# A two-layer decoder trunk on one core: two pairs begun in the first token half instead of one, and half of the affine steps moved to the down stage

## The chip, the core and the metric

The kernel runs on one core of a Trainium2 chip. The metric is the device time of one execution in microseconds (us). TensorE (PE) multiplies matrices into eight accumulator banks; VectorE (DVE) and ScalarE (ACT) read these banks and prepare operands; GpSimd (POOL), SyncE (SP) and ScalarE issue DMAs. Each engine works through its own instructions in order.

## The reference, cut

The input x has 512 tokens of width 1024. Each of two layers mixes tokens (layer 0 by pooling, layer 1 by differential attention) and then runs a gated feed-forward network of inner width 2816.

```
for i in range(DEPTH):                                   # DEPTH = 2
    h = _multiscale_pool(...) if i % 2 == 0 else _diff_attention(...)
    x = _layernorm(ALPHA * x + h, ln_mix_g[i], ln_mix_b[i])
    x = _layernorm(ALPHA * x + _swiglu(x, w_gate[i], w_up[i], w_down[i]), ln_ffn_g[i], ln_ffn_b[i])

def _swiglu(x, w_gate, w_up, w_down):
    return (jax.nn.silu(x @ w_gate) * (x @ w_up)) @ w_down
```

## The kernel before, in words

Every float32 operand is split in two: a **high part**, rounded by a cast on ScalarE (line 670 for gate and up weights), and a **low part**, the rest, taken by a subtraction on VectorE (line 673). Each product is three matmuls: high by high, high by low, low by high. Both parts of a weight chunk of 128x1024 lie in one of six buffer pairs (`WBUFS`), and the raw chunk before it in one of five (`RAWS`); SyncE loads raw chunks in the order of `rows_of_wall`.

The function `ffn(layer, late)` has a gate stage and a down stage.

**Gate stage.** The 2816 inner columns are 22 features of 128. Feature rows k and k + 11 make pair k. Pairs 0 to 2 are computed as six plain features f = 0 to 5, each with a gate product g and an up product u: 24 matmuls of 512 tokens each (lines 160 to 162), or 48 of 256 tokens if the feature is done in two token halves. Pairs 3 to 10 (`SPLIT`) go through `strassen(k)`: seven half products P1, Q5, P6, Q3, P7, P2, Q4 of 24 matmuls of 256 columns (line 877), in place of eight. They work on three banks: A takes P1, P6, P7 and Q4 in turn, C takes Q5 and Q3, B takes P2. Between two of them a bank must be read: P1 is copied from A to B, Q5 from C (line 975) and P6 from A (line 977) by ScalarE; Q3 (line 979) and P7 (line 981) are taken by VectorE. So Q3 waits for the copy of Q5, P7 for the copy of P6, and Q4 for the subtraction of P7. Then follow the gate (silu) and two multiplications into the tile `hid` (lines 994, 995).

The left operands of the seven products are quarters of x or sums of them; `sums_of_x` makes these sums in eight steps that use free rows of `hid`. Four of the seven weight operands are sums of raw chunks (line 667). `ahead(j + n)` writes, after product j, the casts and low parts of all chunks up to j + n - 1; n is the look-ahead.

Two more kinds of work are spread over the gate stage for later. `weight_sums` adds the raw down weights of one feature pair (lines 781, 782), which GpSimd loaded and partly accumulated (lines 775, 776), and ScalarE stores them (line 786). `sum_hidden(k)` makes the sums of `hid` that the down stage needs (lines 807 to 814: four operations of 256 columns, a cast and a low part, then a store). Both are put into the list `behind`, from which `catch_up` takes one step after each product. A pair in `SPARED` has its `sum_hidden` put behind a later pair: {2: 6, 3: 8}.

The first token half of x is ready before the second. A layer therefore begins with products that need only the first half: g and u of the first `EARLY[layer]` features (two in layer 0, one in layer 1), then P1 and P2 of pair 3, which is therefore called **begun** and later has only five products (P6, Q5, P7, Q3, Q4). Among these first products stand the transpositions of the last token blocks (`late`). Then the same features are done for the second half, and the rest follows: the remaining plain features up to 5, then pairs 3 to 10.

The previous layer norm is finished lazily: `affine(n - 1, f)` multiplies a token block of the residual by the norm's gain and adds its bias (lines 238, 239), two VectorE instructions of 1024 columns, behind features 0 to 3. The gain and bias rows lie in a tile of tag `gb`, which afterwards holds down weights of odd pairs.

**Down stage.** The same seven products, in six items each (line 1034, 512 columns), with weights and left operands prepared four and five items ahead. P6 and Q3 add to the second half of the columns of token blocks 0 and 1, P1 and P2 to the first; Q5 and P7 to the second half of blocks 2 and 3, Q4 to the first.

Of the kernel before, what the change touches and what calls it, by code (L numbers as in the profile page):

```python
# [18 lines left out]
P = 128  # L19
S = 512  # L20
# [29 lines left out]
EARLY = (2, 1)  # L50
GATE = ("P1", "Q5", "P6", "Q3", "P7", "P2", "Q4")
SPARED = {2: 6, 3: 8}
# [5 lines left out]
def trunk(ctx, tc, x, wall, pscale, lam_p, subln, table, lng, lnb, band, first, onehot, out):  # L58
# [41 lines left out]
    def rows_of_ffn(layer, c):  # L100
        g = list(range(c, c + 2 * FB))
        e, pair = 2 * EARLY[layer], c + 4 * SPLIT[0]
        return g[:e] + [pair, pair + 3] + g[e:] + list(range(c + 2 * FB, c + 3 * FB))
# [131 lines left out]
    def affine(n, s):  # L235
        z = res[:, s, :]
        gb = gbs[n]
        nc.vector.tensor_tensor(z, z, gb[:, 0, :], op=ALU.mult)
        nc.vector.tensor_tensor(z, z, gb[:, 1, :], op=ALU.add)
# [305 lines left out]
    def ffn(layer, late):  # L545
# [3 lines left out]
        c1 = c0 + 2 * FB + 2  # L549
        down = rows_of_wall[c0] + 2 * FB  # L550
        early = EARLY[layer]
        tt = nc.vector.tensor_tensor
        with tc.tile_pool(name=f"ffn{layer}", bufs=1) as fp:
# [64 lines left out]
            def row(c):  # L618
                return c0 + c + (2 if c >= 2 * early else 0)

            for f in range(2 * SPLIT[0]):
                for i in range(2):
                    plain_chunk((f, i), row(2 * f + i))
                if f == early - 1:
                    plain_chunk((SPLIT[0], 0, "pair"), c0 + 2 * early)
                    plain_chunk((SPLIT[0], 5, "pair"), c0 + 2 * early + 1)
            for k in SPLIT:
                c = [row(4 * k + i) for i in range(4)]
                todo = [(c[0], ()), (c[0], (c[0], c[1])), (c[0], (c[0], c[2])), (c[2], ())]
                todo += [(c[1], (c[1], c[2])), (c[3], ()), (c[0], (c[0], c[3]))]  # L630
                begun = k == SPLIT[0]
# [13 lines left out]
                for w in order_of.split(", "):  # L645
                    steps.append((w[:-2], number[k, int(w[-1]), "pair"]))
            uses = {}
# [68 lines left out]
            def sums_of_x():  # L716

                r0, r1, r2, r3 = spare(4), spare(15), spare(6), spare(17)
# [178 lines left out]
            g3 = fp.tile([P, S], F32, name=f"g3_{layer}")  # L897
            ready_first = 2 * early + 2
            for lo in (0, 256):
                for f in range(early):  # L900
                    for i in range(2):
# [6 lines left out]
                        if not lo and (f, i) in late:  # L908
                            late[f, i]()
# [10 lines left out]
                if not lo:  # L920
                    bankA, bankB = bank(f"A{layer}_{SPLIT[0]}"), bank(f"B{layer}")
                    half_product(bankA, number[SPLIT[0], 0, "pair"], lefts["P1"], True, False, True)
                    if "P1" in late:
                        late["P1"]()
                    nc.scalar.copy(both(g3), both(bankA))
                    next(sums)
                    half_product(bankB, number[SPLIT[0], 5, "pair"], lefts["P2"], True, True)
                    tt(both(g3), both(bankB), both(g3), op=ALU.add)
                    next(sums)

            def plain(f):
# [3 lines left out]
                for i in range(2):  # L935
                    product(a[i], j + i, 0, S)
                    ahead(j + i + 5)
                    if f >= 3:
                        next(sums, None)
                    catch_up()  # L940
                gated(order[f], *a)
                if f < SB:
                    affine(n - 1, f)
                if f % 2:
# [6 lines left out]
            def strassen(k):  # L951
                names = {"P1": "A", "P6": "A", "P7": "A", "Q4": "A", "Q5": "C", "Q3": "C", "P2": "B"}
                begun = k == SPLIT[0]
                banks = {"A": bankA if begun else bank(f"A{layer}_{k}"), "C": bank(f"C{layer}_{k}")}
# [7 lines left out]
                if begun:  # L962
                    g0 = g3
                    nc.scalar.activation(g0, g0, AF.Silu)
                for p in BEGUN if begun else GATE:
# [12 lines left out]
                    elif p == "Q3":  # L978
                        tt(first, acc, first, op=ALU.subtract)  # L979
# [21 lines left out]
            f = early  # L1001
            while f < FB:
                if f // 2 in SPLIT:
                    strassen(f // 2)
                    f += 2
                else:
                    plain(f)
                    f += 1
            if final:
                load_gb(n)  # L1010

# [32 lines left out]
            for p in DOWN:  # L1044
# [7 lines left out]
                for i in range(together):  # L1052
# [13 lines left out]
                    multiply(j, accs, range(2))  # L1066
                for s in range(2):
# [466 lines left out]
    ffn(0, {(1, 0): later(0, 2), "P1": later(0, 3)})  # L1534
    attention()
    ffn(1, {(0, 1): later(2, 3)})
# [108 lines left out]
```

## Time and profile before

| what | value |
|---|---|
| runs | 943.16, 941.47, 939.94 us; median 941.47 |
| profiled execution | 938.56 us |
| its span | 936.8 us |
| granted TensorE clock, mean | 0.998 |
| HBM read, written | 175.50 MB, 36.72 MB |
| gate stage of layer 0, from its first feature to the end of pair 10 | 31.95 to 265.24 us |
| gate stage of layer 1 | 593.33 to 823.79 us |

The span runs from the first to the last instruction of the profiled execution; what lies around it is start and end. Times in the views are microseconds from the span's start unless they are marked ns. A group's row gives the busy time, the mean of one instruction, and the idle time of the engine before it with what ended it.

### The profile page before, as it was taken

The numbers are of one execution on the slowest core, as the hardware profiler recorded it, in microseconds if no ns is written. First come the engines' busy times: TensorE is split into PE (matmuls) and PEld (weight loads), VectorE is DVE, ScalarE is ACT, GpSimd is POOL, SyncE is SP. The second block draws the span as 40 slices with busy tenths as digits, with TensorE's granted clock in tenths as the row PEclk, the third lists the DMA queues.
The fourth block names the chain that finished last, engine by engine and source line by source line (L and its number), as shares of the span: only waits on it lengthen the run. The fifth ranks groups of instructions, "written<-read, shape, count | busy, mean of one in ns | idle before, by whom it ended". The sixth has DMA issues, their size and how long they took to land. (4 is left out here: it accounts for less than half of the span.)

```text
span 936.8 us, 15062 instructions
## 1 busy us (share of the span) xinstructions
PE 923.9 (99%) x5758; PEld 828.1 (88%) x5758; DVE 801.2 (86%) x1172; ACT 517.6 (55%) x826; POOL 127.1 (14%) x152
## 2 busy tenths in 40 slices
PE   9999999999999999999999999999999999999996
PEld 8998899999988888888888888988999999988885
DVE  7979899999988787868989776878899999987778
ACT  6652445544564457676878854833354454564450
POOL 4121111110101201201111100211121110001101
PEclk9999999999999999999999999999999999999999
DMA  8497888886778988966666622595888885888942
GB/s 228 165 307 241 219 294 291 252 272 218 249 247 263 368 265 236 224 198 157 157 146 166 162 79 68 146 343 165 257 281 262 274 263 201 263 285 280 359 163 90
DMA packets 86614, 213.21 MB, mean 228 GB/s; under 512 B 15204, under 2 KB 26724, under 8 KB 86542
## 3 DMA queue, kind: packets, MB, share of 16 engines
q1 hardware_dynamic: 43996, 119.26, 38.2%
q0 software_dynamic: 18768, 58.20, 25.0%
q10 hardware_dynamic: 23778, 34.78, 10.1%
q8 instruction: 45, 0.74, 0.3%
q14 instruction: 27, 0.22, 0.1%
HBM read 175.50 MB, written 36.72 MB: 227 GB/s over the span
## 5 line engine op out<-in xcount | busy, mean ns | idle before, releaser
L667 DVE TENSOR_TENSOR raw<-raw,raw 128x1024 f32<-128x1024 f32 x64 | 78.2, 1222 | 1.5 <-DMA raw<-in_wall 0.5
L134 ACT CAST xs<-hid 128x512 fp32r<-128x512 f32 (+1 forms) x60 | 34.5, 582 | 24.3 <-DVE hid L844 24.3
L135 DVE TENSOR_TENSOR xs<-hid,xs 128x512 fp32r<-128x512 f32 (+1 forms) x60 | 38.3, 642 | 7.8 <-ACT xs L134 7.8
L1273 ACT ACTIVATE p<-p,mn 128x128 f32<-128x128 f32 (+3 forms) x64 | 35.3, 552 | 14.1 <-DVE mn L1268 14.1
L260 ACT ACTIVATE y<-pt,bT,gT 128x128 f32<-128x128 f32 x72 | 27.1, 456 | 24.5 <-PE pt L246 18.5
L775 POOL DMA_DIRECT2D b<-in_wall x20 | 14.0, 705 | 179.6 <-DMA tsum<-b 83.3
L836 POOL DMA_DIRECT2D xs<-ssum x24 | 17.4, 725 | 138.6 <-PE Q L1034 117.4
L975 ACT COPY hid<-C 128x512 f32<-128x512 f32 x16 | 9.4, 588 | 43.7 <-DVE u L807 17.9
L210 POOL TENSOR_TENSOR rs<-rs,mhalf 128x1 f32<-128x1 f32 x16 | 12.9, 806 | 142.1 <-DVE rs L209 97.5
L1268 DVE CUSTOM_DVE_ANT_0 p<-s,bias 128x128 f32<-128x128 f32 (+3 forms) x64 | 28.0, 485 | 1.1 <-PE s L1253 1.1
L775 POOL DMA_DIRECT2D hid<-in_wall x24 | 19.4, 852 | 64.5 <-DMA tsum<-hid 32.5
L724 ACT CAST xs<-hid 128x1024 fp32r<-128x1024 f32 x8 | 8.4, 1051 | 28.0 <-DVE hid L736 17.1
L201 DVE BATCH_NORM_STATS2 st<-res 128x6 f32<-128x512 f32 x32 | 22.2, 694 | 1.1
L135 DVE TENSOR_TENSOR xt<-y,xt 128x512 fp32r<-128x512 f32 x18 | 12.2, 689 | 10.7 <-ACT xt L134 10.7
L776 POOL DMA_DIRECT2D hid<-in_wall x12 | 14.8, 1233 | 48.3 <-DMA hid<-in_wall 48.3
L812 ACT CAST v<-u 128x512 fp32r<-128x512 f32 x22 | 13.6, 616 | 10.7 <-DVE u L810 10.7
L776 POOL DMA_DIRECT2D b<-in_wall x10 | 12.3, 1230 | 51.4 <-DMA b<-in_wall 44.5
L1287 DVE SCALAR_TENSOR_TENSOR p<-p,sm,p 128x128 f32<-128x128 f32 (+3 forms) x32 | 17.7, 552 | 1.1
L979 DVE TENSOR_TENSOR hid<-C,hid 128x512 f32<-128x512 f32 x16 | 11.0, 689 | 8.6 <-PE C L877 8.6
L708 DVE TENSOR_TENSOR hid<-sg,u 128x512 f32<-128x512 f32 x12 | 8.2, 686 | 11.6 <-PE u L162 6.3
L135 POOL TENSOR_TENSOR sql<-sq,sqh 128x512 fp32r<-128x512 f32 x7 | 9.3, 1323 | 60.5 <-ACT sqh L134 60.5
L814 DVE TENSOR_TENSOR v<-u,v 128x512 fp32r<-128x512 f32 x22 | 15.1, 686 | 1.4 <-ACT v L812 0.7
(1220 smaller groups left out, 3627.3 us busy)
## 6 DMA issues: line engine op xcount, KB each, us to landing
raw<-in_wall SPq DMA_DIRECT2D x126, 512.0 KB, 5.1
r<-tsum SPq DMA_DIRECT2D x40, 512.0 KB, 4.5
hid<-in_wall POOLq DMA_DIRECT2D x36, 512.0 KB, 7.8
b<-in_wall POOLq DMA_DIRECT2D x30, 512.0 KB, 7.4
r<-in_wall SPq DMA_DIRECT2D x30, 512.0 KB, 5.7
tsum<-hid ACTq DMA_DIRECT2D x24, 512.0 KB, 5.0
ssum<-v ACTq DMA_DIRECT2D x22, 512.0 KB, 5.2
tsum<-b ACTq DMA_DIRECT2D x20, 512.0 KB, 4.3
```

The source lines that it names most:

```text
L134: nc.scalar.copy(dst_h, src)
L135: (low or nc.vector).tensor_tensor(dst_l, src, dst_h.bitcast(F32), op=ALU.subtract)
L201: nc.vector.bn_stats(stats[n, s][:, d, :], res[:, s, d * 512 : (d + 1) * 512])
L260: nc.scalar.activation(y[:, k, :], pt[:, k * P : (k + 1) * P], AF.Identity, bias=bT[:, n, kk : kk + 1], scale=gT[:, n, kk : kk + 1],)
L667: tt(t, raws[pair[0]], raws[pair[1]], op=ALU.add)
L775: nc.gpsimd.dma_start(out=t[:, j], in_=src[:, j])
L776: nc.gpsimd.dma_start(out=t[:, 0], in_=src[:, :, 1], accum_op=ALU.add)
L814: tt(v[:, :, 1, :], u, v[:, :, 0, :].bitcast(F32), op=ALU.subtract)
L836: nc.gpsimd.dma_start(out=t.bitcast(F32), in_=ssum[:, 0 if p == "P7" else 1, :, r, :])
L1268: nc.vector.tensor_tensor_reduce(out=p, in0=accs[c], in1=biases[h][:, w - 1 :: -1] if w < S else biases[h][:, ::-1], op0=ALU.add, op1=ALU. ...
L1273: nc.scalar.activation(p, p, AF.Exp, bias=mn[:, q, c : c + 1], scale=-1.0, accum_out=sm[:, q, c : c + 1],)
L1287: nc.vector.scalar_tensor_tensor(p0[:, r], p0[:, r], sm[:, q, 0:1], p1[:, r], op0=ALU.mult, op1=ALU.add)
```

## The change

Of the first products, one feature is taken out and one pair put in. `EARLY` becomes (1, 0), and `PRE` = pairs 3 and 4 are both begun: layer 0 starts with g and u of feature 0, then P1 and P2 of pair 3, then of pair 4; layer 1 starts with the four half products of the two pairs alone. P2 of a begun pair now also does all its high parts first. The order behind them is written out: features 0 to 4, pair 3, feature 5, pairs 4 to 10. Features that were halved (feature 1 in layer 0, feature 0 in layer 1) are plain ones now.

`affine` takes half of the columns in the gate stage; the other halves come behind two items of P6 and two of Q3. For that, the gain and bias rows are loaded a second time at the end of the gate stage, and in layer 1 the rows of the last norm are loaded behind the last of these steps instead. The sums of x begin at feature 2 instead of 3 and use rows one lower, so that they share none with the terms of pair 1. The look-ahead becomes 4 in begun pairs and 6 from pair 6 on; the spared sums are those of pairs 3 and 4, put behind pairs 7 and 10, in place of 2 and 3 behind 6 and 8.

```
-EARLY = (2, 1)
+EARLY = (1, 0)
+PRE = SPLIT[:2]
+SUMS = 2
+SPARED = {3: 7, 4: 10}
+ORDER = "f0 f1 f2 f3 f4 p3 f5 p4 p5 p6 p7 p8 p9 p10".split()
+def lookahead(k, p):
+    return 4 if k in PRE else 6 if k > 5 else 4 if p in ("P1", "Q5", "P6") else 5
+AFFINE = {("P6", 2): (0, 1), ("P6", 3): (1, 1), ("Q3", 1): (2, 0), ("Q3", 2): (3, 0)}
-SPARED = {2: 6, 3: 8}
...
-    def affine(n, s):
-        z = res[:, s, :]
+    def affine(n, s, d=None):
+        c = slice(0, D) if d is None else slice(d * 512, (d + 1) * 512)
+        z = res[:, s, c]
...
-                r0, r1, r2, r3 = spare(4), spare(15), spare(6), spare(17)
+                r0, r1, r2, r3 = spare(3), spare(14), spare(5), spare(16)
...
-                    t = rows_of[:, :, 4:6, :]
+                    t = rows_of[:, :, 7:9, :]
...
-            ready_first = 2 * early + 2
+            ready_first = 2 * early + 2 * len(PRE) + (early == 0)
...
                 if not lo:
-                    bankA, bankB = bank(f"A{layer}_{SPLIT[0]}"), bank(f"B{layer}")
-                    half_product(bankA, number[SPLIT[0], 0, "pair"], lefts["P1"], True, False, True)
...
+                    for k in PRE:
+                        pre_a[k], b = bank(f"A{layer}_{k}"), bank(f"B{layer}_{k}")
+                        g = both(pre_g[k])
+                        half_product(pre_a[k], number[k, 0, "pair"], lefts["P1"], True, False, True)
+                        advance(ready_first, True)
+                        turn_late()
+                        nc.scalar.copy(g, both(pre_a[k]))
+                        half_product(b, number[k, 5, "pair"], lefts["P2"], True, True, True)
+                        turn_late()
+                        tt(g, both(b), g, op=ALU.add)
+                        next(sums)
+                    bankB = b
...
-                    product(a[i], j + i, 0, S)
+                    product(a[i], j + i, 0, S, by_part if f == i == 0 else None)
+                    if f >= SUMS:
+                        next(sums, None)
                     ahead(j + i + 5)
-                    if f >= 3:
-                        next(sums, None)
...
-                    affine(n - 1, f)
+                    affine(n - 1, f, f // 2)
-                if f % 2:
+                if f % 2 or f == 0:
                     weight_sums()
...
-                    ahead(j + (4 if begun or p in ("P1", "Q5", "P6") else 5 if k < SPLIT[-1] else 6))
+                    ahead(j + lookahead(k, p))
                     catch_up()
-                    if p == "Q3" and k in SPARED.values():
+                    if p == "Q3":
                         behind.extend(sum_hidden(i) for i in SPARED if SPARED[i] == k)
...
-            if final:
-                load_gb(n)
-
+            load_gb(n - 1)
             while behind:
                 catch_up()
...
                     multiply(j, accs, range(2))
+                    if (p, i) in AFFINE:
+                        affine(n - 1, *AFFINE[p, i])
+                        if final and (p, i) == list(AFFINE)[-1]:
+                            load_gb(n)
...
-    ffn(0, {(1, 0): later(0, 2), "P1": later(0, 3)})
+    ffn(0, {3: later(0, 2), 5: later(0, 3)})
     attention()
-    ffn(1, {(0, 1): later(2, 3)})
+    ffn(1, {2: later(2, 3)})
```

How the instructions move is shown at three places. The first is TensorE at the beginning of layer 0's gate stage; `w2` to `g_5` are weight chunks (h and l their parts), `A_3` and `B_3` the banks of pair 3, `pt` a transposition. Before:

```order
L690 MATMUL u_0_542<-xt,w3h 128x256 x16
L690 MATMUL u_0_542<-xt,w3l 128x256 x8
L690 MATMUL g_1_543<-xt,w4h 128x256 x16
L690 MATMUL g_1_543<-xt,w4l 128x256 x8
L246 MATMUL pt_2_0_630<-ident,res 128x128 x4
L246 MATMUL pt_2_1_631<-ident,res 128x128 x4
L690 MATMUL u_1_544<-xt,w5h 128x256 x16
L690 MATMUL u_1_544<-xt,w5l 128x256 x8
L877 MATMUL A_3_678<-xt,w6h 128x256 x16
L877 MATMUL A_3_678<-xt,w6l 128x256 x8
```

The same place after the change:

```order
L719 MATMUL u_0_542<-xt,w3h 128x256 x16
L719 MATMUL u_0_542<-xt,w3l 128x256 x8
L906 MATMUL A_3_605<-xt,w4h 128x256 x16
L906 MATMUL A_3_605<-xt,w4l 128x256 x8
L266 MATMUL pt_2_0_631<-ident,res 128x128 x4
L266 MATMUL pt_2_1_632<-ident,res 128x128 x4
L906 MATMUL B_3_606<-xt,w5h 128x256 x16
L906 MATMUL B_3_606<-xt,w5l 128x256 x8
L906 MATMUL A_4_682<-xt,w6h 128x256 x16
L906 MATMUL A_4_682<-xt,w6l 128x256 x8
```

The first half of feature 1 gave its place to P1 and P2 of pair 3, and pair 3 its place to pair 4; the transpositions stand where they stood.

The second place is VectorE in pair 7 of layer 0, from the low part of a sum of hidden rows (`v`) to the subtraction of P7 (`A_7`); `C_7` is the bank of Q3. Before:

```order
L814 TENSOR_TENSOR v_6_2124<-u_6_2123,v_6_2124 128x2x256
L979 TENSOR_TENSOR hid_537<-C_7_2090,hid_537 128x2x256
L673 TENSOR_TENSOR g_46l<-raw_1739,g_46h 128x1024
L673 TENSOR_TENSOR g_47l<-raw_1976,g_47h 128x1024
L981 TENSOR_TENSOR hid_537<-hid_537,A_7_2089 128x2x256
```

After the change:

```order
L843 TENSOR_TENSOR v_6_2084<-u_6_2083,v_6_2084 128x2x256
L1019 TENSOR_TENSOR hid_537<-C_7_2048,hid_537 128x2x256
L696 TENSOR_TENSOR raw_1908<-raw_1908,raw_1980 128x1024
L696 TENSOR_TENSOR raw_1980<-raw_1980,raw_2074 128x1024
L702 TENSOR_TENSOR g_48l<-raw_1908,g_48h 128x1024
L1021 TENSOR_TENSOR hid_537<-hid_537,A_7_2047 128x2x256
```

The low parts g_46l and g_47l now come before Q3 is taken, and two sums and a low part of pair 8 stand between Q3 and P7.

The third place is VectorE at the same point of pair 10, the last; `d` are down weights, `xs` a left operand of the down stage. Before:

```order
L979 TENSOR_TENSOR hid_537<-C_10_2810,hid_537 128x2x256
L673 TENSOR_TENSOR g_67l<-raw_2457,g_67h 128x1024
L135 TENSOR_TENSOR d_0l<-r_0_2704,d_0h 128x1024
L135 TENSOR_TENSOR d_1l<-r_1_2775,d_1h 128x1024
L135 TENSOR_TENSOR xs_538<-hid_537,xs_538 128x512 x2
L981 TENSOR_TENSOR hid_537<-hid_537,A_10_2809 128x2x256
```

After the change:

```order
L1019 TENSOR_TENSOR hid_537<-C_10_2767,hid_537 128x2x256
L154 TENSOR_TENSOR d_1l<-r_1_2699,d_1h 128x1024
L154 TENSOR_TENSOR xs_538<-hid_537,xs_538 128x512
L1021 TENSOR_TENSOR hid_537<-hid_537,A_10_2766 128x2x256
L154 TENSOR_TENSOR d_2l<-r_2_2793,d_2h 128x1024
L154 TENSOR_TENSOR xs_538<-hid_537,xs_538 128x512
L836 TENSOR_TENSOR u_4_2934<-hid_537 128x256
L837 TENSOR_TENSOR hid_537<-hid_537 128x256
```

The low parts g_67l and d_0l are made before Q3 is taken; the spared sum of pair 4 (`u_4`) stands behind P7's subtraction.

More of the change, by code (lines that the diff above doesn't have):

```diff
@@ L100, in rows_of_ffn @@
     def rows_of_ffn(layer, c):
-        g = list(range(c, c + 2 * FB))
-        e, pair = 2 * EARLY[layer], c + 4 * SPLIT[0]
-        return g[:e] + [pair, pair + 3] + g[e:] + list(range(c + 2 * FB, c + 3 * FB))
+        g = list(range(c, c + 2 * EARLY[layer]))
+        g += [c + 4 * k + i for k in PRE for i in (0, 3)]
+        for kind, i in units(layer):
+            g += [c + 2 * i + j for j in range(2)] if kind == "f" else [c + 4 * i + j for j in range(4)]
+        return g + list(range(c + 2 * FB, c + 3 * FB))
     order_of_rows = (
@@ L616, in plain_chunk, with rows, plain_chunks, pair_chunks @@
                 step("low", number[key])
[L618 to L628, printed above, removed]
+            row = [c0]
+            def rows(count):
+                row[0] += count
+                return range(row[0] - count, row[0])
+            def plain_chunks(f):
+                for i, c in enumerate(rows(2)):
+                    plain_chunk((f, i), c)
+            def pair_chunks(k):
+                c = rows(4)
                 todo = [(c[0], ()), (c[0], (c[0], c[1])), (c[0], (c[0], c[2])), (c[2], ())]
                 todo += [(c[1], (c[1], c[2])), (c[3], ()), (c[0], (c[0], c[3]))]
-                begun = k == SPLIT[0]
+                begun = k in PRE
                 for p in BEGUN if begun else GATE:
@@ L646, in ffn @@
                     steps.append((w[:-2], number[k, int(w[-1]), "pair"]))
+            for f in range(early):
+                plain_chunks(f)
+            for k in PRE:
+                for m, c in zip((0, 5), rows(2)):
+                    plain_chunk((k, m, "pair"), c)
+            for kind, i in units(layer):
+                (plain_chunks if kind == "f" else pair_chunks)(i)
             uses = {}
```

53 lines of the change are left out of this document (25 added, 28 removed).

## The prediction

> **What bounds the kernel now.** I read the head of the page first, for how full the engines are.
>
> ```profile
> span 936.8 us, 15062 instructions
> PE 923.9 (99%) x5758; PEld 828.1 (88%) x5758; DVE 801.2 (86%) x1172; ACT 517.6 (55%) x826; POOL 127.1 (14%) x152
> ```
>
> TensorE is full, and its granted clock is 1.00 in every stretch shown below. So time can only go where matmuls are removed or made cheaper, or where TensorE waits. The second view is the busy time by stretches. I cut it at the first matmul of each pair as the timeline shows them: layer 0 has pair 3 from 106.87, pair 4 from 121.90 and so on to pair 10, then two stretches of the down stage (Q5's and P6's multiplications); layer 1 has pairs 3, 4, 7, 9 and 10. Columns: length, then busy time and instructions of PE, PEld, DVE, ACT, POOL, the clock, the DMA share and GB/s.
>
> ```profile
> 106.87:121.90 15.03, 14.98 (x121) 14.54 (x120) 13.75 (x16) 4.44 (x8) 1.24 (x1) 1.00 0.96 293
> 121.90:142.89 20.99, 20.41 (x170) 20.21 (x169) 19.93 (x21) 11.64 (x14) 4.17 (x5) 1.00 0.87 281
> 142.89:163.05 20.16, 20.16 (x170) 20.16 (x169) 18.68 (x23) 10.09 (x13) 2.70 (x3) 1.00 0.92 290
> ...
> 183.20:203.80 20.60, 20.44 (x171) 20.24 (x170) 20.39 (x25) 10.53 (x14) 1.91 (x3) 1.00 0.88 273
> ...
> 223.95:244.53 20.58, 20.42 (x171) 20.21 (x170) 20.37 (x25) 10.53 (x14) 2.35 (x3) 1.00 0.70 251
> 244.53:265.24 20.71, 20.41 (x170) 20.21 (x169) 19.66 (x26) 12.66 (x18) 0.00 (x0) 1.00 0.81 254
> 295.19:310.15 14.96, 14.96 (x68) 12.39 (x66) 11.65 (x16) 7.92 (x11) 4.34 (x6) 1.00 0.91 318
> 310.15:325.11 14.96, 14.96 (x68) 12.39 (x66) 9.26 (x11) 5.39 (x7) 3.61 (x5) 1.00 1.00 373
> ...
> 665.98:680.37 14.39, 14.39 (x121) 14.39 (x120) 13.05 (x15) 5.00 (x7) 1.23 (x1) 1.00 0.98 307
> 680.37:700.74 20.37, 20.37 (x171) 20.21 (x169) 18.82 (x20) 11.01 (x14) 4.28 (x6) 1.00 0.86 284
> 741.06:761.63 20.57, 20.41 (x170) 20.20 (x169) 20.36 (x25) 10.60 (x14) 2.70 (x3) 1.00 0.79 255
> 781.79:802.37 20.58, 20.42 (x171) 20.21 (x170) 20.37 (x25) 10.51 (x14) 1.99 (x3) 1.00 0.70 238
> 802.37:823.79 21.42, 20.67 (x171) 20.27 (x170) 19.58 (x26) 12.65 (x18) 0.33 (x1) 1.00 0.80 257
> ```
>
> An undisturbed pair lasts 20.16 us: 7 products of 24 matmuls, 168 in all (the x170 counts neighbours at the borders). What a pair lasts beyond 20.16 (a begun pair of five products: 14.39) is TensorE waiting. In the gate stages that is 0.64 + 0.83 + 0.44 + 0.42 + 0.55 = 2.88 us in layer 0 and 0.21 + 0.41 + 0.42 + 1.26 = 2.30 us in layer 1. The rows also say why: VectorE has 18.7 us of work in a normal pair, and 20.4 in pairs 7 and 9, which follow a spared sum (put behind pairs 6 and 8). VectorE is second in line, with 1.4 us of air per pair. The waits view names whom TensorE waited for:
>
> ```profile
> PE A L877 <- DVE hid L981: 0.9, 2, 0.6
> PE A L877 <- ACT hid L977: 0.8, 5, 0.2
> PE C L877 <- ACT hid L975: 0.6, 1, 0.6
> ```
>
> All are releases of an accumulator bank: VectorE's subtraction of P7 (L981) before Q4, and ScalarE's copies (L977, L975). ScalarE itself is half idle; its copies are late because its queue waits for VectorE, as around pair 7 of layer 0:
>
> ```profile
> 192.95 1.05 ACT L670 CAST g_46h<-raw 128x1024 fp32r<-128x1024 f32 x1 [0.78 <-DVE raw L667]
> 193.90 0.62 ACT L812 CAST v<-u 128x512 fp32r<-128x512 f32 x1
> 194.42 0.58 ACT L977 COPY hid<-A 128x512 f32<-128x512 f32 x1
> ```
>
> The copy of P6 stands behind a cast that waited for VectorE's sum of raw weights.
>
> **The change, part by part.** *Halved features.* The first loop of a layer still has six half products in layer 0 and four in layer 1, and the two transpositions stand at the same places among them. But one feature per layer is now computed on all 512 tokens in 48 matmuls, not in 96 of 256 columns. The wide price is from the chain:
>
> ```profile
> 868.86 14.96 PE Q L1034 x66
> ```
>
> 14.96 / 66 = 226.7 ns for 512 columns; 20.16 / 168 = 120.0 ns for 256. Two narrow ones cost 13.3 ns more than a wide one, and 96 such couples go (48 in each layer): **−1.28 us**, on TensorE itself, so nothing hides it. The Trainium skill, TensorE: Matmul & The Clock Gate, Back-to-back issue gap, gives a warm gap of N / 2.4 ns plus 2.5 ns, by which a couple would save only 2.5 ns; as an estimate from that page the term would be −0.24 us and the forecast 1.04 us later. The rows decide, since they are this kernel's own matmuls with their weight loads.
>
> New weights are wanted 5.8 us earlier after the loop. In layer 1 the first full feature starts where the second half of the first feature started before (first row), and needs the last cast of x (second row):
>
> ```profile
> 605.79 0.28 PE L160 MATMUL g<-xt,w102h 128*128 128x256 f32 x1
> ```
> ```profile
> 603.40 0.62 ACT L134 CAST xt<-y 128x512 fp32r<-128x512 f32 x1
> 603.92 0.58 ACT L925 COPY g<-A 128x512 f32<-128x512 f32 x1
> 604.40 1.05 ACT L670 CAST g_4h<-raw 128x1024 fp32r<-128x1024 f32 x1
> ```
>
> One copy and one weight cast, such as the last two rows (0.58 and 1.05), now precede the casts of x. Even if nothing hides them, the last cast ends 1.63 us later, at 605.65, before 605.79: cost 0. One cast more in front of it would cost 0.9.
>
> *Half of the affine steps.* An affine step has two instructions on 1024 columns; the price of a half is that of the nearest 512-column operation (second row; the third is needed below):
>
> ```profile
> L238 DVE TENSOR_TENSOR res<-res,gb x12: 1217/1220/1221, 59.5 to 646.4; 128x1024 f32<-128x1024 f32 x12
> ```
> ```profile
> 188.18 0.68 DVE L995 TENSOR_TENSOR hid<-sg,hid 128x512 f32<-128x512 f32 x1
> ...
> 190.11 0.42 DVE L807 TENSOR_TENSOR u<-hid 128x256 f32<-128x256 f32 x1
> ```
>
> Before, each gate stage held 8 x 1.22 = 9.8 us of it. Now it holds 8 x 0.68 = 5.4, and the down stage 5.4: 2.7 in P6's multiplication (11.65 becomes 14.4 of 14.96) and 2.7 in Q3's (9.26 becomes 12.0). Weights and left operands are prepared four items of 2.7 us ahead, so I cost this at 0; if that lead is gone, each step holds TensorE by its 1.4 us, 5.4 per layer. The affine rows are loaded once more per layer on SP's queue, in front of down-stage fetches. Those are as far ahead, so 0 too.
>
> *Sums one feature sooner, and a feature between the begun pairs.* In layer 0 VectorE was late for pair 3. Relieved of 4.3 us of affine work and with the sums started a feature earlier, it should have all operands ready: **−0.64**. Behind the begun pair stood pair 4 with 0.83 and 0.21; now it is pair 5 that follows a begun pair, without air in its weights. What held it was this order:
>
> ```profile
> 129.51 0.69 DVE L782 TENSOR_TENSOR hid<-hid 128x512 f32<-128x512 f32 x1
> 130.23 0.37 ACTq L786 DMA_DIRECT2D tsum<-hid  x1
> 130.64 0.59 ACT L975 COPY hid<-C 128x512 f32<-128x512 f32 x1 [3.74 <-DVE hid L782]
> ```
>
> The same order stands in pair 5. VectorE should come there about 0.6 us earlier against TensorE, because a plain feature now stands between the begun pairs, whose 10.9 us hold only two low parts, a gate, a sum of terms and one of hidden rows on VectorE (2.4 + 0.7 + 1.4 + 2.4 = 6.9). I leave 0.2 per layer: −1.04 + 0.4 = **−0.64**.
>
> *Look-ahead of 6 from pair 6 on, spared sums at 7 and 10.* ScalarE's copies now stand ahead of the casts that need new sums, so the pattern of pair 7 goes. Pairs 7 and 9: 0.44 + 0.42 + 0.41 + 0.42 = **−1.69**. In pair 10 the subtraction that Q4 waits for stood behind the low parts g_67l, d_0l, d_1l and two of left operands; now only d_1l and one of a left operand (1.22 + 0.68) stand between it and Q3's. **−1.81**. Against that: in every later pair two sums and one low part now stand between VectorE's evacuation of Q3 and of P7. Their price is here:
>
> ```profile
> 178.31 2.48 DVE L667 TENSOR_TENSOR raw<-raw,raw 128x1024 f32<-128x1024 f32 x2
> 180.71 1.22 DVE L673 TENSOR_TENSOR g_41l<-raw,g_41h 128x1024 fp32r<-128x1024 f32 x1
> ```
> ```profile
> 134.52 0.69 DVE L979 TENSOR_TENSOR hid<-C,hid 128x512 f32<-128x512 f32 x1 [0.92 <-PE C L877]
> ```
>
> From Q3's end (TensorE begins P7 at 134.25): evacuation from +0.27 to +0.96, the three operations to +4.5, P7's subtraction to +5.1, and Q4 is due at +5.76. So 0.5 us of slack is left after 0.15 for the signal. Before, only two low parts (2.3 us) stood there, so the slack was 1.7. Pair 6 gets three more operations (3.6 us) where the look-ahead deepens; 1.4 of air and 1.7 of slack take 3.1, so up to 0.5 can be left: I put +0.3 per layer. Pair 8 follows a spared sum (4 x 0.42 + 0.68 = 2.4 us) with 1.4 of air and 0.5 of slack, so up to 0.5: +0.2 per layer. Together **+1.0**; bounds 0 and 2.0.
>
> Sum: −1.28 − 0.64 − 0.64 − 1.69 − 1.81 + 1.0 = **−5.06 us**. The profiled execution took 938.56 us, its span 936.8 and 1.8 around it; it would become 933.5. It lies 2.9 below the median of the three runs, so from 941.47 the forecast is **936.4 us**.
>
> **The rivals.** *The waits move and do not go.* VectorE's total work hardly falls, so air lost in one pair may return in the next: pairs 5, 6, 8 and 10 of both layers wait about 0.6 each (4.8 us) in place of the 4.54 that pairs 4, 7, 9 and 10 wait now. Left are 1.28 and 0.64, less 0.3: −1.7, **939.8**. For it speaks that a spared pair's 20.4 us of VectorE exceed 20.16, and that pair 10 (19.66) now gets 2.4 more; against it, that VectorE has air in the first features.
>
> *The terms of the last pair are late anyway.* The edit doesn't do what its new order promises if a DMA sets the pace in pair 10:
>
> ```profile
> 801.49 6.42 DMA b<-in_wall
> ```
>
> The chain that ended last begins with this load, which landed at 807.9, 5.5 us into pair 10; VectorE stood before it in order. It now reaches it two operations (2.3 us) later, so most of the wait should be covered. If not, 1.3 remain: −3.8, **937.7**.
>
> *Slower.* The 0.5 us of slack at P7's subtraction fails in all of pairs 6 to 10, because the low part between must await ScalarE's cast of the fresh sum, and that queue holds a v cast and a copy (0.62 + 0.58). With 1.5 us more there, each of 10 pairs waits 1.0: −1.28 − 0.64 − 0.64 − 3.50 + 10 = +3.9, **945.4**. It turns slower from 0.61 us per pair. Against it: at 178.31 the second sum covered the cast and VectorE had no gap.
>
> **How the numbers follow.** Forecast 0.58, moving waits 0.20, late terms 0.10, slower 0.12. The range leaves out the slower case and a little at the fast end: 934.0 (all waits in the gate stages gone, 1.28 + 5.18, and another 1 us of scatter among runs) to 940.9 (the moving waits, with 1.1 for the bounds of the new order). About 0.3%, 2.8 us, can be told from no change here. The forecast and most of the late terms lie beyond it: faster 0.66. The moving waits with the rest: same 0.22. Slower 0.12.
>
> **What would show it.** TensorE should have 96 matmuls fewer, and the second feature of layer 0 and the first of layer 1 should run at 227 ns a matmul. Pair 3 of layer 0 should last 14.4, pairs 7, 9 and 10 about 20.2, pairs 5, 6 and 8 20.2 to 20.5. TensorE should no longer wait for the subtraction of P7 in pair 10. Down-stage multiplications should stay at 14.96. The forecast is wrong if a pair from 6 on lasts over 20.8, if the first full feature of layer 1 starts after 606, or if P6's or Q3's stage grows.

## The result and the profile after

The changed kernel takes **948.68 us** (median of 22 runs, 941.40 to 955.61); the kernel before, on the same chip, 942.63 us (22 runs, 937.83 to 947.88). The ratio is 1.0061, 95% interval 1.0039 to 1.0083: slower by about 5.7 us, where 5 us faster was forecast. The runs also lie further apart than before.

The head of the page of the changed kernel, whose profiled execution took 949.09 us:

```profile
span 947.3 us, 14914 instructions
PE 926.9 (98%) x5662; PEld 824.0 (87%) x5662; DVE 803.5 (85%) x1190; ACT 518.7 (55%) x826; POOL 127.3 (13%) x152
```

The 96 matmuls are gone (5758 to 5662), yet the span is 10.5 us longer. That is more than the medians show, since the profiled execution of before lay 4.1 us under the median of its 22 runs. Busy time by stretches, cut as for the kernel before, in layer 0: pair 3, feature 5, then pairs 4, 5, 6, 7 and 10, then the multiplications of P1, Q5 and P6:

```profile
101.24:115.63 14.39, 14.39 (x121) 14.39 (x120) 11.87 (x15) 5.65 (x8) 3.21 (x4) 1.00 1.02 315
115.63:126.54 10.91, 10.91 (x51) 9.02 (x49) 6.75 (x7) 4.59 (x5) 0.73 (x1) 1.00 0.89 292
126.54:141.38 14.84, 14.62 (x122) 14.45 (x120) 13.54 (x19) 4.82 (x7) 2.64 (x4) 1.00 0.82 290
141.38:162.97 21.59, 20.66 (x170) 20.26 (x169) 20.28 (x21) 11.83 (x14) 4.25 (x6) 1.00 1.00 303
162.97:184.05 21.08, 20.64 (x170) 20.27 (x169) 20.55 (x25) 11.69 (x15) 3.94 (x4) 1.00 0.97 290
184.05:204.21 20.16, 20.16 (x170) 20.16 (x169) 19.18 (x24) 9.82 (x12) 2.70 (x3) 1.00 0.87 263
...
244.71:265.40 20.69, 20.40 (x170) 20.20 (x169) 17.07 (x25) 10.74 (x15) 0.00 (x0) 1.00 0.83 254
265.40:283.49 18.09, 15.55 (x69) 12.25 (x68) 11.31 (x18) 7.92 (x13) 0.00 (x0) 1.00 0.68 220
283.49:298.86 15.37, 15.27 (x68) 12.31 (x66) 14.00 (x19) 8.82 (x14) 0.75 (x1) 1.00 0.73 239
298.86:314.11 15.25, 15.25 (x67) 12.24 (x66) 11.91 (x17) 7.55 (x11) 4.35 (x6) 1.00 0.92 324
```

The same view in layer 1: pairs 4, 5 and 6, then pair 10, P1 and Q5:

```profile
689.50:704.24 14.74, 14.62 (x122) 14.45 (x121) 13.43 (x19) 4.82 (x7) 3.46 (x4) 1.00 0.82 295
704.24:725.84 21.60, 20.67 (x171) 20.26 (x170) 20.35 (x21) 11.83 (x14) 3.44 (x4) 1.00 1.04 330
725.84:746.56 20.72, 20.63 (x171) 20.27 (x170) 20.49 (x25) 11.75 (x15) 3.93 (x4) 1.00 0.82 257
...
807.22:829.22 22.00, 20.67 (x171) 20.27 (x170) 17.07 (x25) 10.73 (x15) 0.00 (x0) 1.00 0.79 241
829.22:847.71 18.49, 15.60 (x68) 12.23 (x67) 11.36 (x18) 7.97 (x13) 0.00 (x0) 1.00 0.67 216
847.71:864.25 16.54, 16.54 (x67) 13.39 (x66) 14.65 (x21) 10.04 (x14) 0.75 (x1) 0.90 0.73 242
```

The largest loss stands where nothing was forecast: P1's multiplications, 14.99 us before, last 18.09 and 18.49. Inside them TensorE is busy for only 15.6 us. In the order of time on ScalarE and its DMA queue (ACTq) in layer 0, with SP's two loads of affine rows ahead of it:

```profile
267.49 0.33 SPq L207 DMA_DIRECT2D gb<-in_lng  x1
267.87 0.42 SPq L208 DMA_DIRECT2D gb<-in_lnb  x1
```
```profile
268.16 0.63 ACT L153 CAST xs<-hid 128x512 fp32r<-128x512 f32 x1
270.82 0.54 ACTq L845 DMA_DIRECT2D ssum<-v  x1
277.31 0.62 ACT L841 CAST v<-u 128x512 fp32r<-128x512 f32 x1 [8.51 <-DMA ssum<-v]
278.69 0.52 ACTq L845 DMA_DIRECT2D ssum<-v  x1
279.25 0.62 ACT L153 CAST d_5h<-r 128x512 fp32r<-128x512 f32 x1 [1.32 <-DVE v L843]
```

At 270.82 the hidden sum of pair 4 is sent off; it was put behind pair 10. At 277.31 pair 10's own hidden sum is cast into the same tile v, of which there is one. So the cast waits until the store has landed, 6.4 us, and every further cast of the down stage (d_5h, then its left operand xs) stands behind it on ScalarE. TensorE runs out of operands at the last item of P1:

```profile
281.17 0.50 PE L1066 MATMUL P<-d_5h,xs 128*128 128x512 f32 x1 [1.98 <-ACT xs L153]
```

### The profile page after: what moved, and what is told of

Its sections match the earlier page's. It is cut to its first block, busy times and chain, and to the rows that moved or that the text cites. A ratio compares the mean times of both kernels' runs of the same rounds, so it can differ in the third digit from the quotient of the medians.

```text
span 947.3 us, 14914 instructions
## 1 busy us (share of the span) xinstructions
PE 926.9 (98%) x5662; PEld 824.0 (87%) x5662; DVE 803.5 (85%) x1190; ACT 518.7 (55%) x826; POOL 127.3 (13%) x152
## 4 chain that ended last, share of the span: by engine, by line
PE 57%; DVE 23%; DMA 8%; issue 6%; ACT 4%; POOL 1%; ACTq 1%; DVEq 0%; POOLq 0%; SPq 0%
PE P L1066 10%; PE Q L1066 6%; PE A L906 6%; DVE raw L696 4%; PE C L906 3%; DMA raw<-in_wall 3%; DMA b<-in_wall 3%; PE va L1220 2%; PE B L906 2%; PE s L1289 2%; PE q L179 2%; PE q L181 2%; PE k L179 2%; PE k L181 2%; PE q L180 2%
## 5 line engine op out<-in xcount | busy, mean ns | idle before, releaser
L753 ACT CAST xs<-hid 128x1024 fp32r<-128x1024 f32 x8 | 8.4, 1050 | 28.5 <-DVE hid L765 15.6
L805 POOL DMA_DIRECT2D hid<-in_wall x12 | 14.8, 1233 | 55.2 <-DMA hid<-in_wall 55.2
L737 DVE TENSOR_TENSOR hid<-sg,u 128x512 f32<-128x512 f32 x12 | 8.2, 686 | 13.5 <-PE u L181 7.3
L259 DVE TENSOR_TENSOR res<-res,gb 128x512 f32<-128x512 f32 (+1 forms) x20 | 16.0, 799 | 0.7
```

## The experiments

Ratios are to the kernel before, in runs on the same chip.

### What holds P1

**A tile of its own for pair 10** (run own_tile). The values of the two begun pairs, no longer needed by then, give their 4 KB to it:

```diff
-                v = fp.tile([P, 2, 2, 256], F32R, tag="v", name=f"v{layer}_{k}", bufs=1)
+                v = pre_v
+                if k < SPLIT[-1]:
+                    v = fp.tile([P, 2, 2, 256], F32R, tag="v", name=f"v{layer}_{k}", bufs=1)
```

> Theory (one tile for two sums): in the changed kernel P1's multiplications last 18.1 and 18.5 us instead of 15.0, because the cast of pair 10's hidden sum waits on ScalarE's queue for the store of pair 4's sum, which sits in the same tile. Pair 10 gets a tile of its own here, and nothing else moves. P1 should last 15.0 in both layers and Q5 15.0 (15.4 and 16.5 before), which takes about 8.5 us off the profiled span of 947.3; what is left against the kernel before is the gate stages and 0.3 in P6, +1.8 us, a ratio of 1.000 to 1.004. Rival (the affine halves and their reloaded rows hold up the preparation of the down stage): P1 stays at 18 or more and the ratio at 1.006.

P1 in both layers:

```profile
266.39:281.38 14.99, 14.99 (x69) 12.39 (x67) 11.60 (x18) 8.66 (x14) 0.00 (x0) 1.00 0.84 265
826.48:841.47 14.99, 14.99 (x68) 12.40 (x67) 11.91 (x18) 8.44 (x14) 0.00 (x0) 1.00 0.78 270
```

Q5 is at 14.96 in both. The ratio is 0.9995 (0.9971 to 1.0018), median 938.83 against 941.07 us. With nothing moved but this tile, 0.66% or 6.2 us come back, which is the whole of the loss within the intervals. The forecast gain does not appear, though: without the stall, the rest of the change is worth nothing that can be told from zero.

**The sum of pair 4 behind pair 9** (run spare_at_9). The edit is `SPARED = {3: 7, 4: 9}`.

> Pair 4's sum is handed over behind pair 9 instead of pair 10; all else is the changed kernel. Theory (one tile for two sums): the store then has a whole pair, 20 us, to land, so P1 and Q5 last 15.0 in both layers, as with a tile of its own; pair 10 has 2.4 us less on VectorE and should lose its 0.5 in layer 0, pair 9 or 10 may get 0.4 each. Ratio to the kernel before 1.000 to 1.004. Rival (affine halves): P1 stays at 18.

P1 is at 14.99 in both layers and pair 10 at 20.20 in both. The ratio is 1.0000 (0.9979 to 1.0021). It is the simplest cure, and the base of the runs below.

**The suspected cause alone, in the kernel before** (run before_spare_at_10). The edit is `SPARED = {2: 6, 3: 10}` in place of `{2: 6, 3: 8}`.

> The kernel before with one number changed: pair 3's spared sum is handed over at pair 10 instead of pair 8. Theory (one tile for two sums): P1's multiplications grow from 15.0 to between 17 and 19 in both layers, and the time by 4 to 8 us (ratio 1.004 to 1.009), although neither the affine halves nor a second begun pair nor the new look-ahead is there. Rival (affine halves, or the new order of weights): the time stays within 1 us of the kernel before.

```profile
267.44:283.23 15.79, 15.29 (x68) 12.29 (x67) 11.31 (x18) 7.93 (x13) 0.00 (x0) 1.00 0.57 195
826.96:845.01 18.05, 15.55 (x69) 12.23 (x68) 11.31 (x18) 7.93 (x13) 0.00 (x0) 1.00 0.68 218
```

The ratio is 1.0067 (1.0042 to 1.0092). P1 grows in both layers, but by 0.8 in layer 0 and 3.1 in layer 1, where 2 to 4 in each were expected. The view by tile `v` names the difference; the first line is layer 0, the second layer 1:

```profile
DMA to landing us min/median/max: 3.8/3.8/3.8
...
DMA to landing us min/median/max: 6.4/6.4/6.4
```

In this kernel only layer 1 loads affine rows at the end of its gate stage, and there the store takes 6.4 us instead of 3.8.

**Whole affine steps in the gate stage** (run whole_affine), so there is no reload in layer 0; in layer 1 the last rows are loaded at this place. The edit, cut:

```diff
-                    affine(n - 1, f, f // 2)
+                    affine(n - 1, f)
...
-            load_gb(n - 1)
+            if final:
+                load_gb(n)
```

> The changed kernel with whole affine steps in the gate stage, as before, and no reloaded rows. Rival (affine halves hold up the down stage): P1 falls from 18 to 15.0 and the time by 6 us or more against the changed kernel (ratio to the kernel before 1.000 or less). Theory (one tile for two sums): P1 stays at 18, P6 falls from 15.25 to 15.0, the gate stage may get 0 to 1 us longer; ratio to the kernel before 1.004 to 1.009.

```profile
270.81:285.80 14.99, 14.99 (x68) 12.40 (x67) 10.68 (x18) 7.75 (x13) 0.00 (x0) 1.00 0.57 185
832.13:849.16 17.03, 15.55 (x68) 12.24 (x67) 9.95 (x17) 7.01 (x12) 0.00 (x0) 1.00 0.62 217
```

Neither theory as written: the stall is gone in the layer without a reload and stays in the other, with the shared tile in both. The ratio is 1.0107 (1.0081 to 1.0134), because P1 still stalls in layer 1 and the whole steps hold pair 3, which lasts 21.31 and 16.38 us. This points to the tile as one half of the cause and the reload beside the store as the other.

**The reload later** (run gb_reload_later), at the start of Q5, with the shared tile kept:

```diff
-            load_gb(n - 1)
             while behind:
...
+                if p == "Q5":
+                    load_gb(n - 1)
```

> The changed kernel, pair 4's sum still handed over at pair 10, but the affine rows are loaded again only at the start of Q5's multiplications and not at the end of the gate stage. Theory (the rows' load makes the store of pair 4's sum slow): where no row load lay in front, the store landed 3.8 to 3.9 us after its issue (whole_affine and before_spare_at_10, layer 0), with it 6.5 to 6.8 (the changed kernel in both layers). So P1 should fall from 18.1 and 18.5 us to between 15.2 and 16.0 in both layers, Q5 to 15.0 to 15.4, and the time by 4 to 7 us against the changed kernel. Rival (the shared tile alone, whatever lies beside the store): P1 stays above 17.5.

P1 and then P6, each in layer 0 and layer 1:

```profile
270.25:285.24 14.99, 14.99 (x69) 12.39 (x68) 10.74 (x18) 7.81 (x13) 0.00 (x0) 1.00 0.56 187
829.21:844.36 15.15, 15.15 (x68) 12.32 (x67) 11.31 (x18) 7.93 (x13) 0.00 (x0) 1.00 0.58 196
300.19:315.88 15.69, 15.55 (x68) 12.24 (x67) 11.94 (x18) 7.98 (x11) 4.35 (x6) 1.00 0.92 331
859.71:875.45 15.74, 15.52 (x67) 12.23 (x66) 11.96 (x18) 7.95 (x11) 4.36 (x6) 1.00 0.93 331
```

P1 is free, or nearly, with the shared tile still there, and the store lands in 3.6 and 3.5 us; P6 pays 0.7 and 0.8 in its place. The ratio is 1.0025 (0.9996 to 1.0055). That is about 3.4 us less than the changed kernel, where 4 to 7 were expected. So the stall of 3 us and more needs both: a sum one pair ahead of another in one tile, and a transfer beside the store that makes its 3.8 us into 6.4. The tile alone cost at most 0.8 us (layer 0 of before_spare_at_10).

### What holds the pairs

**The look-ahead of before** (run look_ahead_as_before), on the kernel of spare_at_9:

```diff
-    return 4 if k in PRE else 6 if k > 5 else 4 if p in ("P1", "Q5", "P6") else 5
+    return 4 if k in PRE or p in ("P1", "Q5", "P6") else 5 if k < SPLIT[-1] else 6
```

> The kernel of spare_at_9 with the look-ahead of the kernel before (4 and 5, 6 in pair 10). Theory (the deeper look-ahead puts two sums and a low part in front of P7's subtraction in pair 6): pair 6 falls from 21.25 and 20.76 us to at most 20.4; in return pairs 8 and 10, which now follow a spared sum, lose 0.4 each and pair 10 a further 0.5 to 1.0. Sum within 1.5 us of spare_at_9. Rival (pair 6 only inherits pair 5's delay): pair 6 stays at 20.7 or more.

Pairs 6, 8 and 10 of layer 0:

```profile
168.56:188.72 20.16, 20.16 (x170) 20.16 (x169) 18.67 (x23) 10.10 (x13) 3.94 (x4) 1.00 0.90 287
208.88:229.47 20.59, 20.42 (x170) 20.22 (x169) 20.38 (x25) 10.53 (x14) 0.00 (x0) 1.00 0.76 237
249.63:271.32 21.69, 20.66 (x170) 20.26 (x169) 21.34 (x28) 13.21 (x19) 0.00 (x0) 1.00 0.78 253
```

Pair 6 waits for nothing, although pair 5 before it lost 1.44, so its wait was the look-ahead's own. Pairs 8 and 10 lose 0.43 and 1.53; no transfer holds VectorE there. The ratio is 1.0015 (0.9992 to 1.0037). Pairs 6, 8 and 10 wait 2.0 and 1.7 us in the two layers, in spare_at_9 1.3 and 0.8: in these profiles the deeper look-ahead has its price in pair 6 and saves about 1.5 us in all, too little for the ratios to show.

**A feature between pair 4 and pair 5** (run feature_before_pair_5), on spare_at_9: the order is f3, p3, f4, p4, f5, p5, and the sums of x start one feature sooner again (`SUMS = 1`).

> The kernel of spare_at_9 with the plain features in another place: pair 3, feature 4, pair 4, feature 5, pair 5 (sums of x one feature sooner still). Theory (pair 5 follows a begun pair at once, and VectorE has no air there, while in feature 5 it stood idle 4 us for raw weights): pair 5 falls from 21.6 us to at most 20.5 in both layers, pair 4 may lose up to 1; 1 to 2.5 us less than spare_at_9. Rival (the order of the operations after a begun pair costs its 1.4 wherever it stands): pair 5 stays above 21.3, or pair 4 loses as much.

Pair 3 of layer 0, pair 5 of layer 0 and pair 5 of layer 1:

```profile
89.56:107.60 18.04, 14.87 (x122) 14.49 (x120) 16.75 (x23) 5.66 (x8) 3.45 (x4) 1.00 0.75 257
143.81:163.96 20.15, 20.15 (x170) 20.15 (x168) 15.99 (x20) 7.95 (x10) 5.07 (x6) 1.00 1.00 328
702.40:722.56 20.16, 20.16 (x170) 20.15 (x169) 16.00 (x20) 7.95 (x10) 4.35 (x6) 1.00 1.00 327
```

Pair 5's 1.45 is gone in both layers and pair 4 waits for nothing; but pair 3 loses 3.64 and 1.12. No transfer holds VectorE ahead of it; that one feature less of time for the same sums is the reason is argued. The ratio is 0.9992 (0.9972 to 1.0011).

**Two more affine halves out of the gate stage** (run more_affine_later), on terms_later (below): `("Q5", 2): (2, 1), ("Q5", 3): (3, 1)` added to the table of halves.

> The kernel of terms_later with two more halves of affine steps moved out of the gate stage into Q5's multiplications, nothing else. Theory: VectorE is 2.7 us further ahead at pair 3, which already waited for nothing in terms_later, and pair 5's 1.4 and pair 6's 0.8 and 0.4 come from the order behind the second begun pair, so they stay: pair 5 21.4 to 21.6 us, and Q5 stays at 15.0 to 15.3. Ratio 0.996 to 0.9985. Rival (VectorE's total work before pair 5 sets it): pair 5 falls below 21 us in both layers.

My theory fails here and the rival holds. Pair 5 falls from 21.6 to 20.4 in both layers:

```profile
139.91:160.27 20.36, 20.36 (x170) 20.20 (x169) 19.31 (x21) 11.06 (x14) 3.43 (x4) 1.00 0.95 298
697.75:718.12 20.37, 20.37 (x171) 20.21 (x169) 18.70 (x20) 11.06 (x14) 3.44 (x4) 1.00 1.04 330
```

So no fixed order costs pair 5 its 1.4: it is VectorE's backlog, and 2.7 us less work ahead of it are enough. Part of the wait moves on in layer 1, where pairs 6 and 8 lose 1.00 and 0.78 in place of 0.39 and 0.18. P6 pays 0.8 per layer. The ratio is 0.9966 (0.9953 to 0.9979).

### Why the runs differ

In the profiles, pair 3 of layer 0 lost 0.64, 0.00, 1.57, 3.27, 3.62, 4.65 and 5.09 us in the kernel before, the changed one, own_tile, spare_at_9, before_spare_at_10, gb_reload_later and look_ahead_as_before. VectorE's row near 70 us goes with it (before, then spare_at_9; its line is L781 in the one and L810 in the other):

```profile
70.67 0.69 DVE L781 TENSOR_TENSOR hid<-hid 128x512 f32<-128x512 f32 x1 [2.12 <-DMA hid<-in_wall]
```
```profile
74.49 0.69 DVE L810 TENSOR_TENSOR hid<-hid 128x512 f32<-128x512 f32 x1 [4.38 <-DMA hid<-in_wall]
```

In the changed kernel's profile that wait is 0, in the other four 2.68, 5.10, 4.69 and 5.18. VectorE waits, in its order, for the accumulating transfer of the second sum of terms.

**That sum one feature later** (run terms_later), on spare_at_9:

```diff
-                if f % 2 or f == 0:
+                if f in (0, 2, 3, 5):
                     weight_sums()
```

> The kernel of spare_at_9 with the second sum of terms of each layer taken one feature later (feature 2 in place of 1). Theory (VectorE, in its order, waits there for the accumulating transfer of those terms, 4.4 us at 74 us of spare_at_9, 2.7 in own_tile, 5.1 in before_spare_at_10, none in the profile of the changed kernel, and pair 3 of layer 0 pays what exceeds 1.1): that wait is gone and pair 3 of layer 0 lasts 14.4 to 14.8 us instead of 17.7; the median falls by 1 to 2.5 us against spare_at_9. Rival (the raw weights are late at pair 3 anyway): pair 3 of layer 0 still loses over 1 us.

The wait is gone and pair 3 lasts 14.39. The median is 938.42 us, the ratio 0.9977 (0.9959 to 0.9995); its interval overlaps that of spare_at_9. Ten runs lie within 3.7 us, where twelve of spare_at_9, on another chip, lay within 7.5.

**The same in the kernel before** (run before_terms_later).

> The kernel before with one call moved: the second sum of terms after feature 2 in place of feature 1. Theory (VectorE waits in its order for the transfer of those terms, and how long differs from run to run; this is where the runs of one kernel differ): VectorE's wait near 70 us is gone, pair 3 of layer 0 loses at most 0.7 us, the median falls by 0.5 to 2 us (ratio 0.998 to 0.9995) and the runs lie closer together (their highest less than 4 us above their lowest, against 8.7 in the 31 runs of the kernel before on this chip). Rival: the runs differ for another reason, their range stays at 7 us or more.

This one tells nothing of the theory: its terms lie in rows that the sums of x overwrite, so those terms are not the reference's, and pair 3 lost 3.1 us to that clash of rows. The ratio is 1.0059 (1.0035 to 1.0082). The next run (before_terms_apart) gives the terms rows of their own:

> The kernel before with the second sum of terms after feature 2 in place of feature 1, and with rows for those terms that the sums of x do not use (7 and 8 of each half, the sums of x one row lower, as in the changed kernel). Theory (VectorE waits in its order for the transfer of those terms, and how long differs from run to run): VectorE's wait near 70 us is gone, pair 3 of layer 0 loses at most 0.7 us, the median falls by 0.5 to 2 us (ratio 0.998 to 0.9995) and the runs lie closer together (highest less than 4 us above the lowest, where the kernel before spreads over 6.5 to 9). Rival: the runs of the kernel before differ for another reason, and their range stays at 6 us or more.

```profile
77.01 0.69 DVE L781 TENSOR_TENSOR hid<-hid 128x512 f32<-128x512 f32 x1
```

There is no wait; pair 3 loses 0.45. Twelve runs lie within 3.6 us, the seventeen of the kernel before beside them within 7.5. The median is 938.85 against 940.27 us, the ratio 0.9987 (0.9972 to 1.0002), so a lower median is not shown. About half of the spread of this kernel's runs goes when VectorE no longer waits for this one transfer.

### All of it together

The run best stands on spare_at_9: terms later, feature 5 behind pair 4, look-ahead 6 from pair 5 on, two more affine halves in Q5.

> All that the runs so far point to, on the kernel of spare_at_9: the second sum of terms one feature later; feature 4 between the begun pairs and feature 5 behind pair 4; look-ahead 6 from pair 5 on, so that its three more operations fall into feature 5; and two more halves of affine steps moved into Q5's multiplications, because with the sums of x a feature earlier still pair 3 lost 3.6 and 1.1 us. Theory (each wait belongs to its own cause): pair 3 loses at most 1 in either layer, pairs 5 to 10 together at most 0.5 per layer, P1 to P6 15.0; the profiled span is 932 to 935, the ratio 0.993 to 0.997. Rival (waits only move): pair 3 or another pair takes 2 us or more per layer and the ratio stays at 0.998 or above.

Pair 3, pairs 5 and 6, pair 10 and P6 of layer 0:

```profile
89.74:105.12 15.38, 14.63 (x122) 14.45 (x121) 14.16 (x19) 5.66 (x8) 1.46 (x2) 1.00 0.98 321
141.32:161.48 20.16, 20.16 (x170) 20.15 (x169) 18.15 (x21) 9.72 (x12) 4.55 (x6) 1.00 1.00 328
161.48:181.64 20.16, 20.16 (x171) 20.16 (x170) 18.67 (x22) 10.31 (x13) 3.56 (x4) 1.00 0.94 278
242.29:262.49 20.20, 20.20 (x171) 20.20 (x169) 19.04 (x28) 12.13 (x18) 0.00 (x0) 1.00 0.88 273
292.44:308.18 15.74, 15.52 (x67) 12.24 (x66) 11.96 (x18) 7.95 (x11) 4.35 (x6) 1.00 0.94 329
```

The median is 935.36 us against 940.33, the ratio 0.9953 (0.9937 to 0.9968), six runs lie within 1.4 us, and the profiled span is 932.9. The rival falls: in the gate stages 1.2 us of waits are left in layer 0 and 0.2 in layer 1. P6 loses 0.8 in each layer, which the theory had at nothing.

## Why the prediction was wrong, step by step

Waits are worked out as in the prediction: what a pair lasts beyond 20.16, a begun one beyond 14.39, a multiplication beyond 14.96 to 14.99. Both layers together, profiled executions:

| step of the prediction | forecast | measured |
|---|---|---|
| halved features | -1.28 | -1.22 |
| pair 3 of layer 0 | -0.64 | -0.64 |
| behind the begun pairs (pairs 4 and 5) | -0.64 | +2.63 |
| pairs 7 and 9 | -1.69 | -1.69 |
| pair 10 | -1.81 | +0.56 |
| new waits in pairs 6 and 8 | +1.0 | +1.84 |
| affine halves and reloaded rows (P1, Q5, P6) | 0 | +8.88 |
| sum | -5.06 | +10.36 |

The span grew by 10.5 us, so next to nothing is left outside these rows.

**Halved features**: right. The wide feature took 10.91 us, where four narrow products take 11.52. By the spacing in the Trainium skill, TensorE: Matmul & The Clock Gate, Back-to-back issue gap, the term was to be -0.24; the measured 10.91 decides for the rows.

**Pair 3**: right in size by chance. In other executions of kernels that hold the same steps it lost up to 5.09, because of the transfer near 70 us. That wait stood in the trace of before (2.12 us), and the prediction did not use it. The affine halves are what pays here. VectorE waited 2.63 us for that transfer in whole_affine and 2.68 in own_tile; pair 3 lost 6.9 us with the whole steps of the one (part of it matmuls at a granted clock of 0.84) and 1.57 with the halves of the other. In layer 1 it lost 2.0 and nothing.

**Pairs 7 and 9**: right. **Pairs 6 and 8**: the right mechanism, within its bounds of 0 and 2.0. P7's subtraction does wait behind two sums and a low part in pair 6; look_ahead_as_before takes it away. (The 0.15 us for the signal in that slack is an allowance; between the end of P7's subtraction and Q4 the rows of before show 0.05 and 0.06.) The slower rival, the same in all of pairs 6 to 10, did not come: pairs 7 and 9 lost nothing.

**Behind the begun pairs**: wrong. The step that failed is "VectorE should come there about 0.6 us earlier against TensorE, because a plain feature now stands between the begun pairs". It counted 6.9 us of work in the feature's 10.9 and took the rest for air that VectorE could use to get ahead. The changed trace shows 6.75 us of work there, and behind it this:

```profile
118.13 1.23 DVE L696 TENSOR_TENSOR raw<-raw,raw 128x1024 f32<-128x1024 f32 x1 [3.36 <-DMA raw<-in_wall]
```

VectorE stood idle for raw weights, at a DMA share of 1.02 in the pair ahead. Pair 4, now begun too, then took 13.5 of VectorE's 14.8 us, and pair 5 follows at once. Putting feature 5 behind pair 4, or taking 2.7 us off VectorE, ended it. That the late weights themselves cause it was not tried, but one profile bears it out: in layer 1 of look_ahead_as_before, with the same order here, VectorE waited 1.95 us for them, and pair 4 lost nothing and pair 5 0.40.

**Pair 10**: the time is wrong, and the step that failed is "so most of the wait should be covered". The new order does what it was to do, as own_tile shows, which keeps it: its pair 10 of layer 0, first line below, waits for nothing. (In whole_affine it lasts 20.16 in both layers.) In the profile of the changed kernel VectorE waits, second and third line, for the transfer of the last terms in layer 0 and in layer 1:

```profile
246.23:266.39 20.16, 20.16 (x170) 20.16 (x169) 18.34 (x27) 11.86 (x17) 0.00 (x0) 1.00 0.82 263
```
```profile
250.74 0.69 DVE L810 TENSOR_TENSOR b<-b 128x512 f32<-128x512 f32 x1 [2.47 <-DMA b<-in_wall]
```
```profile
814.56 0.69 DVE L810 TENSOR_TENSOR b<-b 128x512 f32<-128x512 f32 x1 [3.78 <-DMA b<-in_wall]
```

That is the rival "the terms of the last pair are late anyway", which put 1.3 us; 0.53 and 1.84 were lost. VectorE came to this operation 3.6 us into the pair, where it came after 3.9 before, and not 2.3 later as the prediction had it; the terms landed later too (in layer 1 7.3 us into the pair, before 5.5). The wait differs between executions: layer 1 of own_tile lost 1.41 to it, spare_at_9, where the sum of pair 4 stands ahead of this operation, 0.04. Pair 4's hidden sum, which stands behind P7's subtraction in pair 10, is not the cause.

**Affine halves and reload**: wrong, and the step that decided the sign. The step that failed is "Those are as far ahead, so 0 too". It priced the reload by who waits for the rows, and the profiles show nobody who does. The loss came from what the reload runs beside, the store of pair 4's sum. And `SPARED = {3: 7, 4: 10}` was priced as 2.4 us on VectorE; that pair 10 makes a sum of its own, in the same tile, was not looked at. 6.6 us of the 8.88 are P1's stall; 2.0 are Q5, 1.58 of it matmuls at half rate after the stall in layer 1 (below). The halves themselves cost nothing that can be told: Q3 stays at 14.96, and P6's 0.29 comes without halves too (15.25 in layer 0 of before_spare_at_10). The two rows of the down stage in the prediction are those of P6 and Q3, as its sum uses them, and not of Q5 and P6 as its label says.

**The rivals**: none of them has the stall of P1. The moving waits come nearest in the gate stages, where pairs 5, 6, 8 and 10 wait 7.1 us in place of the 4.8 that this rival put; 2.4 of them are pair 10's transfer.

## What to carry to other kernels

When a step is moved next to another of its kind, look up how many buffers its result has and what empties them. If it is a transfer, price it at the place it moves to, with the other transfers that run there, and count everything that stands behind the waiting instruction on its engine. A short idle time of an engine in a full stage is not air until the trace says what it waits for. Before a wait is laid to the order of operations, look at other executions with the same order: pair 10's wait came and went with a transfer. Runs of one kernel that differ by 1% may hang on one transfer that an engine awaits in its order; taking that operation later brought the range from 7.5 to 3.6 us here.

## What the runs showed of the hardware

At the start of P1, a store of 512 KB on ScalarE's queue landed 3.5 to 3.8 us after its issue with no loads of affine rows ahead of it (gb_reload_later, layer 0 of whole_affine and of before_spare_at_10) and 6.4 to 6.8 us after it with two such loads issued on SP's queue 3.3 to 3.6 us ahead. This agrees with the Trainium skill, DMA: Bandwidth & Descriptors, Queues, rings and completion order, by which a DMA engine takes turns between the queues that have work for it.

In layer 1, after stops of 2.34 and 0.56 us at the end of P1, the first of Q5's matmuls ran 427 ns apart in place of 226.7. The stretch shows the granted clock (0.57):

```profile
847.71:851.50 3.79, 3.79 (x11) 2.88 (x10) 3.79 (x6) 3.79 (x6) 0.00 (x0) 0.57 0.78 260
```

In layer 0, after stops of 1.98 and 0.56 us, the clock stayed at 1.00. Three more stops stand at P7 of pair 3 in layer 0: after 2.79 us (spare_at_9) the clock stayed at 1.00, after 3.10 (gb_reload_later) and 4.25 us (whole_affine) it was 0.63 over the next 4.0 and 0.50 over the next 3.6 us. So the matmuls behind a stall can cost extra, here 1.58 us behind a loss of 3.5; what decides it for stops of 2 to 3 us is not shown.
